# A hybrid encoder layer on one core: the order of the first gated units, the tiles for copies of x, and the queues of the far stretch

## The chip, the cores and the metric

The kernel runs on one core of a Trainium2 chip. The metric is the time of one execution on the device, in microseconds (us). The core has a matrix engine (TensorE, PE in the profile), three engines for the rest (VectorE or DVE, ScalarE or ACT, GpSimd or POOL) and SyncE (SP), which here only issues transfers. A transfer (DMA) is issued by the queue of one engine, in that queue's order, and moved by 16 DMA engines that all queues share.

## The reference

One layer over 2048 tokens of width 1024, all in float32:

```python
y = rmsnorm(x, norm_mix_g) @ w_in            # 512 q, 512 k, 512 v, 512 a, 512 g
att  = dilated_sliding_attention(rotary(q), rotary(k), v)   # 8 heads of 64; dilations 1, 4, 16
conv = silu(layernorm(conv31(a * sigmoid(g))))              # depthwise, 31 taps
h = x + concat(att, conv) @ w_out
xq, xk, xv = rmsnorm(h) @ w_xq, rmsnorm(mem) @ w_xk, rmsnorm(mem) @ w_xv   # 256 memory rows
h = h + cross_attention(xq, xk, xv) @ w_xo                  # 4 heads of 256
h = h + square(relu(rmsnorm(h) @ w_up)) @ w_down            # 4096 wide
out = rmsnorm(h, norm_final_g)
```

The attention takes three patterns (windows of 128, 512 and 2048 tokens at dilations 1, 4 and 16), each a softmax over a band, and joins them by their log-denominators.

## The kernel before, in words

Tokens are taken in four blocks of 512 (`n` or `p` = 0 to 3), channels in tiles of 128. Products are made exact enough by splitting each operand into a high and a low part: three matmuls (lines 263 to 265, `mm3`) for each product, into one PSUM bank of 128 x 512.

The order in which each engine takes its instructions is made by a planner: it takes the program's order as priority and issues what its own timing says is ready, so work may come earlier than it is written. Python generators interleave the stages (`weave(main, (side, rate))` takes `rate` steps of a side for each step of the main one; `pipeline` runs weight loads and splits of later units ahead). `after(stack, name)`, and `behind` and `pinned` that use it, put what is traced inside behind the last instruction kept under that name: "pe" is the last matmul, "dve" a VectorE instruction, "sumsq" ScalarE's sum of squares, "x0_7" the ScalarE cast (line 406) of tile 7 of block 0. The edge is made by `tc.issue_after` and orders instructions within a queue; it waits for no result.

**The first stage.** `xprep(sp, n)` (line 386) loads a block of x in its natural layout, sums squares on ScalarE (line 375), makes the factor of the norm, and then, for each of eight channel tiles, transposes it on TensorE (line 400), copies it out (VectorE, line 402, into a tile `xts` with three buffers), writes the copy to DRAM (`xscr`, on SyncE's queue; it is wanted far later), scales it (`xv`, VectorE, line 405), casts it to f16 (`xh`, ScalarE, line 406) and subtracts (`xl`, GpSimd, line 407). `glu_first` (line 631) runs the first gated pair, channel tile 0 of g and a, over blocks 0 and 1. Per unit it loads 128 columns of `w_in`, squares them, scales, casts, subtracts (`wscale` and `scaled_split`: lines 202, 219, 220, 221), and runs 24 matmuls per block (8 channel tiles by 3). The other pairs for blocks 0 and 1 come from `glu`, then the q and k units (`lin_qk`, which need the scales made in `qkscale` from all of w_in's q and k columns) and the v unit (`lin_v`). `edges` writes zeros to the ends of two arrays in DRAM, `memory` prepares the 256 memory rows.

**The far stretch** (about 450 to 770 us) runs attention for block 0, all three patterns, of which the one with dilation 16 (`att_far`, line 1000 on) covers all tokens. Beside it `filler` runs the gated pairs for blocks 2 and 3 and `Matrices`, which makes the cross-attention's k and v projections (`proj`), the scores' matrices (`turn`, `score`) and the back projections (`back`), each from weights loaded in order into two buffers (`raw_m`, line 461). Attention parks its parts in DRAM (`oscr`) and reads them again in `combine`. Weights and attention's keys, queries and values are loaded on SyncE's queue; results (`kscr`/`vscr` of the projections, `ascr`, `bscr`, `oscr`) are written on GpSimd's. After 124 steps of attention (50 and 74) the rest of the filler is drained, then `backs`, the back projections and the first two w_out tiles, run alone; then `post(0)` starts, with attention's last steps woven in.

Of the kernel before, what the change touches and what calls it, by code (L numbers as in the profile page):

```python
# [21 lines left out]
P = 128  # L22
# [25 lines left out]
def hybrid_layer(ctx, tc, A, out):  # L48
# [338 lines left out]
    def xprep(sp, n):  # L387
        xtiles(n)
        nat = [load_nat(sp, A["x"][0, 512 * n + P * j:512 * n + P * (j + 1), :], f"xn{n}_{j}", q=nc.gpsimd if n > 1 else None) for j in range(4)]
        yield  # L390
        r = rstd_nat(sp, nat, f"x{n}")
        rb = ps("c", f"rb{n}")
        bcast_rows(rb, r, 4)
        rbs = sp.tile([P, 512], F32, tag="rbs", name=f"rbs{n}", bufs=1)
        ACT.copy(rbs, rb)
        yield
        for k in range(KC):
            pt = ps("a", f"xt{n}_{k}")
            for j in range(4):
                PE.transpose(pt[:, j * P:(j + 1) * P], nat_cols(nat[j], k), ident)  # L400
            xt = sp.tile([P, 512], F32, tag="xt", name=f"xts{n}_{k}", bufs=3)
            DVE.tensor_copy(xt, pt)
            dma(xscr[k][:, 512 * n:512 * (n + 1)], xt)
            xv = sp.tile([P, 512], F32, tag="xv", name=f"xv{n}_{k}", bufs=2)
            DVE.scalar_tensor_tensor(xv, pt, gmix[:, k:k + 1], rbs, op0=ALU.mult, op1=ALU.mult)
            last[f"x{n}_{k}"] = ACT.copy(XH_[k, n], xv)
            POOL.tensor_tensor(XL_[k, n], xv, XH_[k, n], op=ALU.subtract)
            yield
# [5 lines left out]
    def memory(sp):  # L414
# [7 lines left out]
        ACT.copy(gm, pm[:, 0:8])  # L422
        mh, ml = ([sp.tile([P, 4, NMEM], F32R, tag=f"m{q}{i}", name=f"m{q}{i}") for i in range(2)] for q in "hl")
        for k2 in range(KC // 2):
# [18 lines left out]
    class Matrices:  # L443
# [8 lines left out]
        def load(self, i):  # L452
            if i >= 32:
                return
            raw = wp.tile([P, 8, P] if i < 24 else [P, 2, 512], F32, tag="raw", name=f"raw_m{i}", bufs=2)
            if i < 24:
                src = wcols((w_xk, w_xv, w_xq)[i // KC], i % KC * P)
            else:
                h, nh = divmod(i - 24, 2)
                src = w_xo[256 * h:256 * h + 256, 512 * nh:512 * nh + 512].rearrange("(e p) m -> p e m", p=P)  # L460
            dma(raw, src)
            self.ring[i] = raw
# [20 lines left out]
        def gather(self, x, h):  # L483
            t = self.part(f"mvm{h}", f"{x}t{h}", (P, 2, 2, NMEM))
            for q in range(2):
                dma(f(t[:, q]), f(pscr[x][q, 2 * h:2 * h + 2].rearrange("e p m -> p e m")))
            return t

        def proj(self, i):
# [16 lines left out]
            for q in range(2):  # L506
                dma(f(pscr[x][q, j]), f(t[q]), nc.gpsimd)
            if i == 15:
# [22 lines left out]
        def score(self, h):  # L531
            kt, wt = self.kt, self.wt
            for k2 in range(4):
                pt = ps("mm", f"pa{h}{k2}")
                for q in range(2):
                    k = 2 * k2 + q
                    for e in range(2):
# [5 lines left out]
                                  self.rbm.unsqueeze(1).to_broadcast([P, 2, NMEM]), op=ALU.mult)  # L543
                dma(ascr[h // 2, :, 2 * k2:2 * k2 + 2, h % 2, :], e3, nc.gpsimd)
                if k2 == 3:
# [3 lines left out]
        def back(self, i):  # L549
# [4 lines left out]
            for mc in range(2):  # L554
# [4 lines left out]
                if mc == 0:  # L559
# [3 lines left out]
                dma(bscr[4 * nh:4 * nh + 4, :, 2 * h + mc, :].rearrange("m p c -> p m c"),  # L563
                    ev.rearrange("p (m c) -> p m c", c=P), nc.gpsimd)
                yield
# [33 lines left out]
    def glu(c, ns, fine=False):  # L599
# [4 lines left out]
        def unit(x, c0):  # L604
            raw = wlin("raw", f"{x}{c}{ns[0]}")
            dma(raw, wcols(w_in, c0))
            yield
# [22 lines left out]

    def glu_first(c, ns):

        raw, w, sig = {}, {}, {}
        c0 = {"g": 3 * DATT + DCONV + c * P, "a": 3 * DATT + c * P}
        for x in "ga":
            raw[x] = wlin("raw", f"{x}{c}{ns[0]}")
            dma(raw[x], wcols(w_in, c0[x]))
            yield
        for x in "ga":
            yield from wscale(raw[x], f"{x}{c}", 1 if x == "g" else 0)  # L640
            w[x] = wlin("whi", f"{x}{c}{ns[0]}"), wlin("wlo", f"{x}{c}{ns[0]}")
            scaled_split(raw[x], kept_scale[f"{x}{c}"][0], *w[x], POOL)
            yield
        DVE.tensor_scalar(cwu[:, c], cw[:, c], kept_scale[f"a{c}"][1], None, op0=ALU.mult)
        for n in ns:
            for x in "ga":
                pt = ps("mm", "lin")
                for _ in linear_steps(pt, *w[x], n):
                    yield
                if x == "g":  # L650
                    sig = t2(f"sig{c}_{n}")
                    ACT.activation(sig, pt, AF.Tanh, scale=kept_scale[f"g{c}"][1])
                else:
                    u = t2(f"u{c}_{n}")
                    last["dve"] = DVE.scalar_tensor_tensor(u, sig, 1.0, pt, op0=ALU.add, op1=ALU.mult)
                    dma(uscr[c][:, 15 + 512 * n:15 + 512 * (n + 1)], u)
                yield
# [24 lines left out]
    def lin_v(hook):  # L682
# [4 lines left out]
        def load(e):  # L687
            raws[e] = wp.tile([P, 8, P], F32, tag="raw", name=f"raw_v{e}", bufs=2)
            dma(raws[e], wcols(w_in, 2 * DATT + P * e))

# [203 lines left out]
    with ExitStack() as st:  # L894
        sp = pool("stage", stack=st)
        setup()
        pair = glu_first(0, (0, 1))
        x0, x1 = xprep(sp, 0), xprep(sp, 1)
        next(x0)
        next(pair)  # L900
        next(x1)
        next(pair)
        next(x0)
        for _ in range(3):
            behind("sumsq", pair)
        drain(x0)
        for _ in range(3):
            behind("x0_7", pair)
        early01 = (0, 1)
        units = [pair] + [u for c in range(1, 4) for u in glu(c, early01)]  # L910
        units += [lin_qk(isq, c) for c in ("r", 0, 1, 2) for isq in (False, True)]
# [93 lines left out]
    def att_far(p2_, h, k, vt, q, start=0):  # L1005
# [7 lines left out]
        def unit(rq):  # L1013
# [96 lines left out]
    def att_units(p, far, then):  # L1110
# [25 lines left out]
        def unit(pr, hh, pat, g, k, q_, opt, o0):  # L1136
# [139 lines left out]
    with ExitStack() as st:  # L1276
# [55 lines left out]

        drain(pinned(backs(), "pe"))

# [637 lines left out]
```

## Time and profile before

| | us |
|---|---|
| median of 3 runs | 2873.29 |
| fastest and slowest of these | 2869.66 and 2874.86 |
| the profiled execution | 2869.13 |
| its span in the trace | 2867.3 |
| TensorE busy in the span | 2709.2 |
| VectorE, ScalarE, GpSimd busy | 1902.0, 1274.5, 538.1 |

A group of the profile reads: line, engine, operation, the tile written and the tiles read, shapes, count, then busy time and mean nanoseconds of one, then the engine's idle time just before them and what ended it. A row of the timeline is start, duration, engine, line, operation, and in brackets the idle time before it with its cause. A row of the waits is who waited for whom: us in total, times, longest. SPq and POOLq are the issues of DMAs on SyncE's and GpSimd's queues. Rows by stages give, for each stretch, busy time and count of each engine, the granted TensorE clock, the share of the DMA engines and GB/s.

### The profile page before, as it was taken

How to read it: one execution, taken by the hardware profiler on the slowest of the kernel's cores; microseconds unless marked ns; L12 is line 12 of the kernel's file. 1: busy time of each engine (PE TensorE's matmuls, PEld its weight loads, DVE VectorE, ACT ScalarE, POOL GpSimd, SP SyncE). 2: the span in 40 equal slices, each digit the busy share in tenths (PEclk: the TensorE clock that was granted, in tenths of full speed). 3: DMA queues.
4: the chain of work that ended last, by engine and by line, in shares of the span. 5: the costliest groups of instructions: out<-in, count | busy, mean ns of one | idle time of the engine just before them, and what ended most of it. 6: DMA issues, size and time to landing. Idle time of an engine off the chain costs nothing.

```text
span 2867.3 us, 40621 instructions
## 1 busy us (share of the span) xinstructions
PE 2709.2 (94%) x14783; PEld 2082.4 (73%) x14783; DVE 1902.0 (66%) x3475; ACT 1274.5 (44%) x2171; POOL 538.1 (19%) x744
## 2 busy tenths in 40 slices
PE   4999999879789999999999999999999999999998
PEld 2544447666577787878888888888888788878877
DVE  3548835555379876568897478866474776666665
ACT  4753215645435433433554534454343544444335
POOL 3545302332200221220210201111020122200000
PEclk8999999999899999999999999999999999999999
DMA  8665537776643666676547766775533554485553
GB/s 239 196 171 113 141 103 216 209 220 181 218 144 118 211 224 204 220 230 213 184 144 239 238 216 219 223 231 176 182 120 121 169 202 164 151 306 162 173 180 103
DMA packets 488096, 535.68 MB, mean 187 GB/s; under 512 B 81637, under 2 KB 361817, under 8 KB 487896
## 3 DMA queue, kind: packets, MB, share of 16 engines
q1 hardware_dynamic: 457360, 434.94, 50.5%
q0 software_dynamic: 28688, 94.82, 9.2%
q10 hardware_dynamic: 1848, 3.33, 0.3%
q8 instruction: 116, 1.90, 0.3%
q14 instruction: 84, 0.69, 0.1%
HBM read 384.46 MB, written 148.52 MB: 186 GB/s over the span
## 4 chain that ended last, share of the span: by engine, by line
PE 65%; issue 10%; DVE 8%; DMA 8%; ACT 3%; POOL 3%; SPq 2%; POOLq 0%; ACTq 0%; DVEq 0%
PE b L1670 7%; PE dn L263 4%; PE dn L264 4%; PE dn L265 4%; PE up L263 3%; PE up L265 3%; PE up L264 3%; PE pt L962 2%; SPq L57 2%; DVE cacc L280 2%; PE s L1155 2%; PE x L264 1%; PE x L263 1%; PE x L265 1%; PE lin L263 1%
## 5 line engine op out<-in xcount | busy, mean ns | idle before, releaser
L280 DVE SCALAR_TENSOR_TENSOR cacc<-cu,cwu,cacc 128x512 f32<-128x512 f32 x480 | 396.8, 828 | 6.4
L956 ACT ACTIVATE sm<-sm,o 128x256 f32<-128x256 f32 (+1 forms) x384 | 160.4, 467 | 125.2 <-DVE o L955 124.9
L263 PE MATMUL dn<-hhh,whi_d 128*128 128x512 f32 x512 | 201.6, 404 | 3.6 <-ACT hhh L1507 2.6
L263 PE MATMUL up<-mh,whi_u 128*128 128x512 f32 x512 | 203.9, 398 | 0.0
L264 PE MATMUL dn<-hhl,whi_d 128*128 128x512 f32 x512 | 199.7, 393 | 0.8 <-DVE hhl L1508 0.8
L265 PE MATMUL up<-mh,wlo_u 128*128 128x512 f32 x512 | 200.0, 391 | 0.0
L264 PE MATMUL up<-ml,whi_u 128*128 128x512 f32 x512 | 199.7, 390 | 0.0
L265 PE MATMUL dn<-hhh,wlo_d 128*128 128x512 f32 x512 | 198.9, 391 | 0.0
L955 DVE CUSTOM_DVE_ANT_0 sm<-s,mask 128x256 f32<-128x256 f32 (+1 forms) x384 | 127.2, 375 | 35.2 <-PE s L1155 13.7
L966 DVE TENSOR_TENSOR pl<-pt,ph 128x512 f16<-128x512 f32 x160 | 109.8, 686 | 58.2 <-ACT ph L965 57.6
L1522 DVE TENSOR_TENSOR h<-h,dn 128x512 f32<-128x512 f32 x128 | 86.4, 684 | 70.8 <-PE dn L265 70.3
L241 POOL TENSOR_TENSOR nr<-st_v,mhalf 128x4 f32<-128x4 f32 x12 | 13.5, 1127 | 629.1 <-DVE st_v L237 629.0
L965 ACT CAST ph<-pt 128x512 f16<-128x512 f32 x160 | 92.6, 579 | 79.8 <-PE pt L962 79.0
L263 PEld LDWEIGHTS dn<-hhh,whi_d 128*128 128x128 f32 x512 | 95.4, 188 | 22.6 <-ACT hhh L1507 3.6
L265 PEld LDWEIGHTS up<-mh,wlo_u 128*128 128x128 f32 x512 | 96.1, 188 | 20.5
L265 PEld LDWEIGHTS dn<-hhh,wlo_d 128*128 128x128 f32 x512 | 96.2, 188 | 20.1
L264 PEld LDWEIGHTS dn<-hhl,whi_d 128*128 128x128 f32 x512 | 96.4, 188 | 19.3 <-DVE hhl L1508 1.6
L264 PEld LDWEIGHTS up<-ml,whi_u 128*128 128x128 f32 x512 | 96.3, 188 | 18.6
L263 PEld LDWEIGHTS up<-mh,whi_u 128*128 128x128 f32 x512 | 96.2, 188 | 18.5
L263 PE MATMUL o<-cath,whi_o 128*128 128x512 f32 x256 | 102.9, 403 | 1.5 <-ACT cath L1104 0.8
L263 PE MATMUL x<-pth,whi_b 128*128 128x512 f32 x256 | 101.1, 401 | 2.4 <-ACT xp L1431 1.5
L263 PE MATMUL xs<-whi_a,yh 128*128 128x512 f32 x256 | 102.3, 401 | 0.0
(586 smaller groups left out, 7965.6 us busy)
## 6 DMA issues: line engine op xcount, KB each, us to landing
raw_u<-in_w_up_dram SPq DMA_DIRECT2D x64, 512.0 KB
raw_d<-in_w_down_dram SPq DMA_DIRECT2D x64, 512.0 KB
k<-kscr SPq DMA_DIRECT2D x32, 640.0 KB
raw_o<-in_w_out_dram SPq DMA_DIRECT2D x32, 512.0 KB
raw_a<-ascr SPq DMA_DIRECT2D x32, 512.0 KB
raw_b<-bscr SPq DMA_DIRECT2D x32, 512.0 KB
lou<-wlo_u POOLq DMA_DIRECT2D x32, 512.0 KB, 5.6
lod<-wlo_d POOLq DMA_DIRECT2D x32, 512.0 KB, 5.6
```

The lines of the kernel that those rows point to most:

```text
L57: (q or nc.sync).dma_start(o, i)
L263: PE.matmul(o, lh, rh, start=first, stop=False)
L264: PE.matmul(o, lh, rl, start=False, stop=False)
L265: last["pe"] = PE.matmul(o, ll, rh, start=False, stop=end)
L280: DVE.scalar_tensor_tensor(acc, u[:, t:t + 512], cwu[:, c, t:t + 1], acc, op0=ALU.mult, op1=ALU.add)
L955: last["dve"] = DVE.tensor_tensor_reduce(dst, so, mask[:, 256 * m:256 * m + nk], 1.0, 3e38, ALU.add, ALU.min, mn)
L956: last["act"] = ACT.activation(dst, dst, AF.Exp, bias=mn, scale=-1.0)
L962: last["pe"] = PE.transpose(pt[:, j, :], sm[:, j, :], ident)
L965: ACT.copy(ph, pt)
L966: DVE.tensor_tensor(pl, pt, ph, op=ALU.subtract)
L1522: last["dve"] = DVE.tensor_tensor(hs[m], hs[m], pt, op=ALU.add)
L1670: PE.matmul(o, w[i][:, k, :], Y[b][q][k], start=first and k + x == 0, stop=k == 3 and x == 2, skip_group_check=not first)
```

## The change

In the first stage, `glu_first` takes both of the first two pairs (g0, a0, g1, a1): it asks for the four weight tiles, the first of them ahead of the first block of x, and runs all four units over block 0 before any runs over block 1. The fourth weight tile lies in a buffer of the `weights` pool, the second pair's split parts in tiles of the stage's own pool, and the memory rows' parts move from that pool to the `weights` pool's split buffers to make room. `xts` has eight buffers instead of three. The steps and rates of the interleaving are set anew; `qkscale` is pinned behind "x1_7"; `edges` is put behind "x3_7", the v weights' and the mask's loads behind "pe".

In the far stretch, the loads of `raw_m`, of the gated pairs for blocks 2 and 3, and of the projections' gathered parts go to GpSimd's queue, and the writes of the projections, scores, back projections and attention's parts to SyncE's. `backs` is woven with attention at 0.55 steps for each of its own instead of running alone.

```diff
-            xt = sp.tile([P, 512], F32, tag="xt", name=f"xts{n}_{k}", bufs=3)
+            xt = sp.tile([P, 512], F32, tag="xt", name=f"xts{n}_{k}", bufs=8)
...
-        mh, ml = ([sp.tile([P, 4, NMEM], F32R, tag=f"m{q}{i}", name=f"m{q}{i}") for i in range(2)] for q in "hl")
+        mh, ml = ([wp.tile([P, 4, NMEM], F32R, tag=f"w{q}", name=f"m{q}{i}", bufs=2) for i in range(2)]
+                  for q in ("hi", "lo"))
...
-            dma(raw, src)
+            dma(raw, src, nc.gpsimd)
...
-                dma(f(t[:, q]), f(pscr[x][q, 2 * h:2 * h + 2].rearrange("e p m -> p e m")))
+                dma(f(t[:, q]), f(pscr[x][q, 2 * h:2 * h + 2].rearrange("e p m -> p e m")), nc.gpsimd)
...
-                dma(f(pscr[x][q, j]), f(t[q]), nc.gpsimd)
+                dma(f(pscr[x][q, j]), f(t[q]))
...
-                dma(ascr[h // 2, :, 2 * k2:2 * k2 + 2, h % 2, :], e3, nc.gpsimd)
+                dma(ascr[h // 2, :, 2 * k2:2 * k2 + 2, h % 2, :], e3)
...
-                    ev.rearrange("p (m c) -> p m c", c=P), nc.gpsimd)
+                    ev.rearrange("p (m c) -> p m c", c=P))
...
-            dma(raw, wcols(w_in, c0))
+            dma(raw, wcols(w_in, c0), nc.gpsimd if fine else None)
...
+    def glu_first(sp, ns):
+
+        units = [(x, c) for c in range(2) for x in "ga"]
+        raw, w, sig = {}, {}, {}
+        for x, c in units:
+            nm = f"{x}{c}"
+            raw[nm] = (wp.tile([P, 8, P], F32, tag="raw", name=f"fraw_{nm}", bufs=2) if nm == "a1" else
+                       wlin("raw", f"{nm}0"))
+            dma(raw[nm], wcols(w_in, 3 * DATT + c * P + (DCONV if x == "g" else 0)))
+            yield
+        for x, c in units:
+            nm = f"{x}{c}"
+            yield from wscale(raw[nm], nm, 1 if x == "g" else 0)
+            w[nm] = [sp.tile([P, 8, P], F16, tag=f"f{q}{nm}", name=f"f{q}_{nm}") if c else wlin(f"w{q}", f"{nm}0")
+                     for q in ("hi", "lo")]
+            scaled_split(raw[nm], kept_scale[nm][0], *w[nm], POOL)
+            if x == "a":
+                DVE.tensor_scalar(cwu[:, c], cw[:, c], kept_scale[nm][1], None, op0=ALU.mult)
+            yield
         for n in ns:
-            for x in "ga":
+            for x, c in units:
                 pt = ps("mm", "lin")
-                for _ in linear_steps(pt, *w[x], n):
+                for _ in linear_steps(pt, *w[f"{x}{c}"], n):
                     yield
...
-            dma(raws[e], wcols(w_in, 2 * DATT + P * e))
+            with ExitStack() as st:
+                after(st, "pe")
+                dma(raws[e], wcols(w_in, 2 * DATT + P * e))
...
-        pair = glu_first(0, (0, 1))
+        four = glu_first(sp, (0, 1))
         x0, x1 = xprep(sp, 0), xprep(sp, 1)
+        next(four)
         next(x0)
-        next(pair)
+        next(four)
         next(x1)
-        next(pair)
+        next(four)
+        next(four)
         next(x0)
         for _ in range(3):
-            behind("sumsq", pair)
+            behind("sumsq", four)
         drain(x0)
         for _ in range(3):
-            behind("x0_7", pair)
+            behind("x0_3", four)
+        behind("x0_5", x1)
+        for _ in range(6):
+            behind("sumsq", four)
         early01 = (0, 1)
-        units = [pair] + [u for c in range(1, 4) for u in glu(c, early01)]
+        units = [four] + [u for c in range(2, 4) for u in glu(c, early01)]
...
-        drain(islice(steps, 10))
-        behind("x0_3", x1)
-        weave(islice(steps, 6), (x1, 1.4))
+        drain(islice(steps, 6))
+        weave(islice(steps, 24), (x1, 0.5))
         drain(x1)
         later = pinned(chain(xprep(sp, 2), xprep(sp, 3), memory(sp)), "x1_7")
-        qks = qkscale()
-        weave(islice(steps, 16), (later, 0.25), (qks, 0.25))
-        weave(islice(steps, 11), (later, 2.4), (qks, 0.7))
+        qks = pinned(qkscale(), "x1_7")
+        weave(islice(steps, 34), (later, 0.4), (qks, 0.2))
+        weave(islice(steps, 7), (later, 2.4), (qks, 0.7))
         drain(later, qks)
-    edges()
+    with ExitStack() as st0:
+        after(st0, "x3_7")
+        edges()
...
-    dma(mask, A["masks"])
+    with ExitStack() as st0:
+        after(st0, "pe")
+        dma(mask, A["masks"])
...
-                dma(oscr[pr][1].rearrange("(p r) (h e) -> p r h e", r=16, h=2)[:, 4 * rq - 4:4 * rq + 4, hh], o2,
-                    nc.gpsimd)
+                dma(oscr[pr][1].rearrange("(p r) (h e) -> p r h e", r=16, h=2)[:, 4 * rq - 4:4 * rq + 4, hh], o2)
...
-                    os_.rearrange("p b h e -> p b (h e)"), nc.gpsimd if far else nc.scalar)
+                    os_.rearrange("p b h e -> p b (h e)"), None if far else nc.scalar)
...
-        drain(pinned(backs(), "pe"))
+        weave(pinned(backs(), "pe"), (first, 0.55))
```

More of the change, by code (lines that the diff above doesn't have):

```diff
@@ L629, in glu @@
         return unit("g", 3 * DATT + DCONV + c * P), unit("a", 3 * DATT + c * P)
-    def glu_first(c, ns):
+    def glu_first(sp, ns):
+        units = [(x, c) for c in range(2) for x in "ga"]
         raw, w, sig = {}, {}, {}
-        c0 = {"g": 3 * DATT + DCONV + c * P, "a": 3 * DATT + c * P}
-        for x in "ga":
-            raw[x] = wlin("raw", f"{x}{c}{ns[0]}")
-            dma(raw[x], wcols(w_in, c0[x]))
-            yield
[L639 to L642, printed above, removed]
+        for x, c in units:
[3 more added lines that the diff above has]
+            dma(raw[nm], wcols(w_in, 3 * DATT + c * P + (DCONV if x == "g" else 0)))
+            yield
+        for x, c in units:
[6 more added lines that the diff above has]
+                DVE.tensor_scalar(cwu[:, c], cw[:, c], kept_scale[nm][1], None, op0=ALU.mult)
             yield
-        DVE.tensor_scalar(cwu[:, c], cw[:, c], kept_scale[f"a{c}"][1], None, op0=ALU.mult)
         for n in ns:
-            for x in "ga":
+            for x, c in units:
                 pt = ps("mm", "lin")
-                for _ in linear_steps(pt, *w[x], n):
+                for _ in linear_steps(pt, *w[f"{x}{c}"], n):
                     yield
```

## The prediction

> **What bounds the kernel now.** I read the page first, then the busy time by stages, then the waits of the engine that is busiest, and then the order of time where that engine stood still. Busy columns are TensorE, its weight loads, VectorE, ScalarE, GpSimd; after them the granted clock, the DMA share and GB/s.
>
> ```profile
> span 2867.3 us, 40621 instructions
> ```
>
> ```profile
> 24.00:84.00 60.00, 36.97 (x168) 20.07 (x166) 26.29 (x55) 30.73 (x66) 31.86 (x36) 0.83 0.79 221
> 84.00:100.00 16.00, 13.47 (x62) 6.61 (x61) 5.97 (x10) 13.87 (x36) 6.75 (x6) 0.89 0.57 170
> 100.00:165.00 65.00, 60.54 (x312) 31.85 (x311) 35.80 (x81) 41.08 (x72) 30.34 (x28) 0.97 0.68 181
> 165.00:450.00 285.00, 274.90 (x1294) 129.89 (x1293) 177.83 (x217) 81.00 (x106) 100.08 (x122) 0.99 0.54 144
> 450.00:720.00 270.00, 236.05 (x2269) 189.19 (x2268) 154.72 (x549) 153.03 (x345) 82.60 (x121) 0.96 0.71 197
> 720.00:800.00 80.00, 54.36 (x287) 41.05 (x284) 29.71 (x70) 30.81 (x51) 13.48 (x18) 0.86 0.73 226
> ```
>
> TensorE bounds it nearly everywhere. The holes are in the two stages that the change edits: 23.0 us from 24 to 84 us, and 34.0 plus 25.6 us in the far stretch (450 to 800). Between 100 and 450 us only 14.6 of 350 us are idle: whatever is won ahead of that can be kept there, since TensorE only has to start its queue sooner. Time is won by filling holes, not by removing arithmetic: the change removes no matmul.
>
> The early hole, in order of time on VectorE, TensorE and SyncE's queue:
>
> ```profile
> 44.86 0.69 DVE L402 COPY xts<-xt 128x512 f32<-128x512 f32 x1 [15.41 <-DMA xscr<-xts]
> ...
> 46.35 1.94 PE L400 MATMUL xt<-ident,xn 128*128 128x128 f32 x8 [13.80 <-DVE xv L405]
> ...
> 21.42 13.20 SPq L57 DMA_DIRECT2D uscr<-zero  x8
> 34.66 0.43 SPq L57 DMA_DIRECT2D raw_v<-in_w_in_dram  x1
> 37.31 0.33 SPq L57 DMA_DIRECT2D mask<-in_masks_dram  x1
> 37.74 0.38 SPq L57 DMA_DIRECT2D xscr<-xts  x1
> ```
>
> VectorE's sixth copy of x needs the tile of the third, there being three. That tile's write to DRAM stands on SyncE's queue behind eight writes of zeros, a v weight and the mask, is issued at 37.74 and lands shortly before 44.86. VectorE waits 15.41 us, and TensorE, behind VectorE, 13.80.
>
> **The change part by part.** *Eight tiles for the copies.* All eight copies of x's first 512 tokens then have a tile of their own, so the 13.80 us go, whatever SyncE's queue does. What is late next: the second 512 tokens reuse the tiles, and their third copy needs the write of 37.74; it comes no sooner than about 44, so little is left of that wait. Term: -13.8.
>
> *Two gated pairs over tokens 0 to 511 first, then over 512 to 1023.* What TensorE does per matmul at full clock, and what the other engines need per tile and per unit of weights:
>
> ```profile
> 78.61 0.38 PE L265 MATMUL lin<-xh,lwlo_a 128*128 128x512 f16 x1
> 78.82 0.60 PE L400 MATMUL xt<-ident,xn 128*128 128x128 f32 x4
> 79.26 0.38 PE L263 MATMUL lin<-xh,lwhi_g 128*128 128x512 f16 x1
> ```
>
> ```profile
> 24.00:84.00 60.00, 28.20 (x98) 0.69 (x1) 1.06 (x2) 0.83 0.79 221
> ```
>
> ```profile
> L407 POOL TENSOR_TENSOR xl<-xv,xh 128x512 f16<-128x512 f32 x16 | 18.4, 1163 | 17.4 <-ACT xh L406 17.2
> L400 PE MATMUL xt<-ident,xn 128*128 128x128 f32 x64 | 12.5, 337 | 15.8 <-DVE xv L405 15.7
> L405 DVE SCALAR_TENSOR_TENSOR xv<-xt,gmix,rbs 128x512 f32<-128x512 f32 x16 | 11.6, 744 | 4.3 <-ACT rbs L395 2.3 <-POOL xl L407 1.9
> L402 DVE COPY xts<-xt 128x512 f32<-128x512 f32 x16 | 11.0, 688 | 25.8 <-DMA xscr<-xts 15.4 <-PE xt L400 10.3
> ...
> L219 ACT ACTIVATE lraw_g<-lraw_g,wscl 128x1024 f32<-128x1024 f32 x2 | 2.3, 1141 | 1.3 <-DVE sqv_g L189 1.3
> ...
> L221 POOL TENSOR_TENSOR lwlo_a<-lraw_a,lwhi_a 128x1024 f16<-128x1024 f32 x1 | 2.1, 2128 | 0.6 <-ACT lwhi_a L220 0.6
> ```
>
> From 78.61 to 78.82 a matmul takes 0.21 us, and four transposes 0.44. The second of these fences counts the gated matmuls alone: 98 by 84 us, beside 64 transposes. After the change 96 gated matmuls (four units of 24) need only the first 512 tokens: 96 x 0.21 + 16 x 0.44 = 27.2 us. The first gated matmul came at 24.54; one of the x loads will be later for the weight ahead of it, so I start at 25.5 and reach 52.7. Holes that stay: the second unit's weights are squared, scaled, cast and subtracted (some 1.1 us each on ScalarE, 2.1 on GpSimd, about 5.5 in all) behind x's fourth tile, and the third and fourth units' behind the sums of the next tokens; I put 7 us on them. VectorE's own 16 tiles at 0.74 + 0.69 are 22.9 us from about 22, which ends at 45 and is no bound; GpSimd's 16 x 1.16 + 4 x 2.13 = 27.1 us ends near 52 and is close to one. So the state of 84 us is reached near 60: 24 us sooner, of which 13.8 are counted, 10 more at best and none at worst. I take -7, since every engine is then near its sum. *Weights ahead of x*: half a megabyte at the 221 GB/s of that stage is 2.4 us for the first x load (bounds 0 and +2.4, the sums of squares having slack elsewhere): +1.
>
> *The q and k scales' sums, held on ScalarE behind the second 512 tokens' last tile.* They are also asked for later in the order of the work.
>
> ```profile
> L740 ACT ACTIVATE qks<-qks x16: 616/628/632, 72.2 to 133.8; 128x512 f32<-128x512 f32 x16
> ```
>
> They spread over 62 us now. Begun at 60 and spread alike they end at 122; the q and k units that need them would like to start 20 us sooner than now. Nothing at best, +8 if they slip by an eighth of their spread: +2.
>
> *Three edits that I cost at nothing: edge zeros behind "x3_7", mask and v weights behind "pe".* Such a name holds a ScalarE or TensorE instruction, while these blocks issue on SyncE and VectorE. The profile shows what such a hold does, since the preparation of x's third 512 tokens is held behind "x1_7" already:
>
> ```profile
> 26.14 0.72 POOL L57 DMA_DIRECT2D xn<-in_x_dram  x1
> ...
> 76.26 0.62 ACT L406 CAST xh<-xv 128x512 f16<-128x512 f32 x1 [0.64 <-DVE xv L405]
> 76.78 0.62 ACT L375 ACTIVATE junk<-xn 128x512 bf16<-128x512 f32 x1
> ```
>
> The cast at 76.26 is x1_7. ScalarE's sums follow it at once, but the loads were issued on GpSimd's queue 50 us ahead of it: a hold binds only its own engine. The zeros, mask and v weights go on filling SyncE's early gaps. If the holds did bind, 13.2 us of SyncE's queue would move from 21 us to near 130: -3 to +5.
>
> *The far stretch's queues.* 40 weight loads (32 of cross-attention, 8 gated) and 16 gathers go to GpSimd's queue; 32 projections, 16 score, 16 back and 20 attention writes go to SyncE's. The two longest waits of GpSimd's queue there, two of the stretches in which TensorE idles (columns as above), and TensorE's own waits from 720 on:
>
> ```profile
> POOL oscr L57 <- ACT o L1034: 50.5, 9, 13.1
> POOL bscr L57 <- ACT eb L562: 34.3, 13, 8.9
> ```
>
> ```profile
> 610.00:620.00 10.00, 2.73 (x10) 1.86 (x11) 3.81 (x11) 2.14 (x5) 1.43 (x8) 0.50 0.69 178
> ...
> 790.00:800.00 10.00, 1.83 (x16) 1.15 (x16) 8.93 (x29) 1.60 (x4) 0.00 (x0) 0.71 0.76 216
> ```
>
> ```profile
> PE pb L263 <- ACT eb L562: 17.0, 6, 6.6
> PE opt L970 <- DMA v<-vtok: 6.2, 1, 6.2
> ```
>
> ```profile
> DMA to landing us min/median/max: 2.7/4.6/8.1
> ```
>
> The last row is the time from issue to landing of the back projections' writes. For it: a weight no longer queues on SyncE behind the loads of the concatenation. Against it: 84.8 us of waiting for results (and more for the scores) move in front of attention's key, query and value loads. GpSimd waited in the same order and with the same slack, and loses as many issues as it gains, so its combines (which run in order behind its DMAs) see one kind of wait for another. Bounds: -13 (the ten microseconds at 610 and one value wait, less than whole) to +50.5; nearest row is TensorE's single value wait of 6.2 us, small and already there, so 0.
>
> The trace gives the DMA share as 0.71 in this stretch and 0.73 in the next. The Trainium skill, DMA: Bandwidth & Descriptors, section Rules for kernel authors, says that spreading transfers over issuing engines brings no bandwidth and saves only issue time; by that rule this term is 0 as well, and the head-of-queue waits are what can make it differ.
>
> *Attention's last steps woven into the back projections at 0.55 per step.* About 25 steps take some 13 of attention, which is nearly all that is left. TensorE idles 17.0 us in the back projections, waiting for ScalarE, which waits for the write of two tiles before (landing 4.6 us); attention fills part of it, and the 8.2 us hole at 790, where the last combine and a value load are awaited, loses the combine. Bounds 0 and -25; half of the hole and a third of the waits is -10.
>
> Sum: -13.8 - 7 + 1 + 2 + 0 - 10 = -27.8. The profiled execution took 2869.13 (its span and 1.83 around it), so 2841.3; the median of the runs is 4.2 above that execution, so 2845.
>
> **The rivals.** *A, slower: SyncE holds attention's loads behind its new writes.* Place: 450 to 720. The waits for the far output (50.5) stand at the head of SyncE's queue, and each delays the next head's keys and the single-buffered values. If all of it reached TensorE: 2845 + 50.5 = 2895. It decides from 28 us, 55% of that row. For it: the queue is served in order. Against: TensorE is busy for 236 of 270 us there, which leaves slack, and these writes are ready before the next head starts.
>
> *B: the early gain is lost again.* If q and k start no sooner, because the scale sums, ScalarE (13.87 busy of 16 us at 84) or GpSimd set the pace, about 6 of the 18 stay, and with 0 to -10 from the back projections: 2857 to 2867.
>
> *C, about even or slower: weights on GpSimd land late.* A transfer from there lands between 2.7 and 8.1 us after issue; 3.5 above the median on each of 24 later matrices is 84, of which two buffers hide at least half: 2845 + 42 = 2887.
>
> The Trainium skill, SBUF — State Buffer, section SBUF: two separate sides, names a cause for C: some VectorE copies lock GpSimd out while it writes descriptors. No run here shows it yet.
>
> *D, faster: the swap also fills the idle stretches of the far stage:* 2845 - 13 - 5 = 2827.
>
> **How the numbers follow.** The forecast 2845 (2834 to 2857) has 0.42, D 0.15, B 0.20 (a third of it within 0.2%, 5.7 us, about what a measurement can tell from no change), A 0.13, C 0.07, smaller mixtures 0.03, of which 0.01 is within 0.2%. Faster: 0.42 + 0.15 + 0.13 + 0.02 = 0.72; same 0.08; slower 0.20. The range from 2822 to 2884 leaves out A, half of C and the end of D, about 0.2.
>
> **What would show it.** Right: no wait of VectorE for xscr before 60 us; x1_7 cast near 60 instead of 76.26; 98 gated matmuls by 60; zeros still on SyncE ahead of 60; TensorE idle under 12 us in the back projections. Wrong: value or key waits of TensorE of tens of microseconds from 450 to 720 (A), ScalarE waiting for raw_m (C), or idle TensorE between 100 and 200 (B).

## The result, and the profile after

The changed kernel takes 2827.32 us (median of 4 runs, 2822.73 to 2827.61), against 2871.47 for the kernel before beside it (4 runs, 2868.08 to 2874.86): a ratio of 0.9842, 95% interval 0.9825 to 0.986. That is some 45 us less, where 28 were forecast: near the fast end of the range from 2822 to 2884, and faster than the 2834 to 2857 around the forecast.

The span and the busy time by stages, in the same six stages as in the prediction:

```profile
span 2825.5 us, 40587 instructions
...
24.00:84.00 60.00, 50.35 (x247) 26.12 (x248) 28.69 (x66) 39.60 (x82) 37.35 (x38) 0.97 0.87 246
84.00:100.00 16.00, 16.00 (x85) 8.43 (x84) 7.20 (x19) 15.97 (x42) 6.70 (x7) 1.00 0.63 210
100.00:165.00 65.00, 56.43 (x273) 29.71 (x271) 35.80 (x61) 36.53 (x57) 30.09 (x32) 0.92 0.77 190
165.00:450.00 285.00, 278.17 (x1392) 137.28 (x1391) 183.68 (x261) 87.46 (x133) 108.04 (x123) 0.99 0.53 145
450.00:720.00 270.00, 233.01 (x2207) 186.42 (x2206) 152.55 (x528) 151.79 (x335) 70.71 (x98) 0.94 0.76 211
720.00:800.00 80.00, 73.31 (x379) 59.36 (x378) 54.84 (x95) 40.73 (x63) 1.44 (x2) 0.96 0.73 214
```

TensorE is busy for 50.35 of the first 60 us instead of 36.97, with 247 matmuls instead of 168; part of it is lost again between 100 and 165 (8.6 us idle instead of 4.5). The last row compares different work, since all of it begins earlier. For the far stretch it is better to compare landmarks: the first start of attention's transposes, of the back projections, of the output projection, and of the score products behind it. They are read from rows like these two, of before and of after (count, shortest, median and longest ns, first and last start):

```profile
L962 PE MATMUL pt<-ident,sm x640: 269/272/477, 456.8 to 1947.8; 128*128 128x128 f32 x160
```

```profile
L978 PE MATMUL pt<-ident,sm x640: 269/273/422, 438.5 to 1901.7; 128*128 128x128 f32 x160
```

| kernel (label) | first `pt` | first `pb` | first `o` | first `xs` | span | `pt` to `pb` | `pb` to `xs` |
|---|---|---|---|---|---|---|---|
| before | 456.8 | 721.7 | 768.2 | 834.6 | 2867.3 | 264.9 | 112.9 |
| after | 438.5 | 690.5 | 746.6 | 791.8 | 2825.5 | 252.0 | 101.3 |
| e1_early | 440.3 | 702.7 | 751.6 | 816.1 | 2845.1 | 262.4 | 113.4 |
| e2_tiles8 | 448.5 | 712.7 | 760.0 | 825.1 | 2859.9 | 264.2 | 112.4 |
| e3_queues | 453.6 | 707.0 | 752.5 | 817.4 | 2853.9 | 253.4 | 110.4 |
| e4_weave | 461.4 | 726.3 | 787.2 | 832.3 | 2867.4 | 264.9 | 106.0 |
| e5_loads | 457.0 | 721.8 | 766.2 | 831.6 | 2862.9 | 264.8 | 109.8 |
| e6_writes | 452.1 | 698.7 | 741.0 | 806.1 | 2843.1 | 246.6 | 107.4 |
| e7_after_tiles3 | 442.2 | 691.8 | 748.1 | 793.3 | 2827.7 | 249.6 | 101.5 |
| e8_after_bscr_act | 435.1 | 689.7 | 746.3 | 795.5 | 2834.2 | 254.6 | 105.8 |
| e9_writes_only | 439.3 | 685.8 | 742.6 | 790.4 | 2824.6 | 246.5 | 104.6 |
| e10_writes_bind | 445.8 | 689.9 | 744.8 | 789.8 | 2827.6 | 244.1 | 99.9 |
| e11_oscr | 458.2 | 720.4 | 764.8 | 830.2 | 2867.0 | 262.2 | 109.8 |
| e12_xwrites | 458.0 | 714.2 | 758.7 | 823.5 | 2855.6 | 256.2 | 109.3 |

So of the change's 42.8 us by the score products, 18.3 are there when attention starts, 12.9 are won up to the back projections, and 11.6 from there on. After that nothing more is won: the span is 41.8 us shorter. Each row is one profiled execution. Single landmarks of kernels that share their first stage differ by up to 9 us (452.1 to 461.4 where that stage was not edited), and the stretch behind the score products, where no edit lies, takes 2029.0 to 2038.7 us; so a few microseconds are decided by the ratios.

### The profile page after: what moved, and what is told of

It is laid out like the page before. It is cut to its first block, busy times and chain, and to the rows that moved or that the text cites. A ratio compares the mean times of both kernels' runs of the same rounds, so it can differ in the third digit from the quotient of the medians.

```text
span 2825.5 us, 40587 instructions
## 1 busy us (share of the span) xinstructions
PE 2697.4 (95%) x14783; PEld 2075.6 (73%) x14783; DVE 1898.2 (67%) x3475; ACT 1272.6 (45%) x2171; POOL 525.7 (19%) x716
## 4 chain that ended last, share of the span: by engine, by line
PE 69%; DMA 9%; issue 8%; DVE 6%; ACT 4%; POOL 2%; SPq 1%; ACTq 0%; POOLq 0%; DVEq 0%
PE b L1685 7%; PE dn L263 4%; PE dn L264 4%; PE dn L265 4%; PE up L263 3%; PE up L265 3%; PE up L264 3%; PE lin L263 2%; PE lin L265 2%; PE lin L264 2%; PE pt L978 2%; PE s L1170 2%; SPq L57 1%; PE x L264 1%; PE x L263 1%
## 5 line engine op out<-in xcount | busy, mean ns | idle before, releaser
L265 PEld LDWEIGHTS up<-mh,wlo_u 128*128 128x128 f32 x512 | 96.2, 188 | 20.4
```

The lines of the kernel that those rows point to most:

```text
L265: last["pe"] = PE.matmul(o, ll, rh, start=False, stop=end)
```

## The experiments

**The first stage alone.** First all of the first stage's edits on the kernel before, then only the tiles of the copies.

```diff
+            xt = sp.tile([P, 512], F32, tag="xt", name=f"xts{n}_{k}", bufs=8)
+        four = glu_first(sp, (0, 1))
...
```

> The first stage of the change alone (two pairs, weights ahead of x, eight copy tiles, the new interleaving), with the far stretch's queues and the back projections as before. My theory: attention's first transpose comes about 18 us sooner (456.8 before, 438.5 in the changed kernel) and all of it reaches the end: 2871 - 18 = 2853. Rival (the far stretch takes it back, since its DMA waits set its pace): 2862 or more.

```diff
-            xt = sp.tile([P, 512], F32, tag="xt", name=f"xts{n}_{k}", bufs=3)
+            xt = sp.tile([P, 512], F32, tag="xt", name=f"xts{n}_{k}", bufs=8)
```

> Only the eight tiles for the copies of x, on the kernel before. My theory by the prediction's term: 13.8 us less, 2857, since TensorE's 13.80 us wait goes and the work that follows is bound by TensorE. Rival: the wait is replaced by others (one pair has only 48 matmuls per block to fill with), 5 us or less, 2866 to 2871.

Measured: the whole first stage 0.9932 (0.9914 to 0.995), about -19.5 us; the eight tiles alone 0.9958 (0.9942 to 0.9974), about -12. VectorE's longest wait up to 100 us and the busy time of the early stretch of e2_tiles8, then the busy time of e1_early, whose first row is TensorE alone up to 69 us:

```profile
DVE xts L402 <- PE xt L400: 22.7, 14, 7.4
```

```profile
24.00:84.00 60.00, 44.81 (x193) 23.23 (x192) 29.56 (x61) 40.27 (x89) 36.09 (x38) 0.83 0.84 246
```

```profile
24.00:69.00 45.00, 35.43 (x167) 0.96 0.86 230
...
24.00:84.00 60.00, 50.43 (x244) 26.25 (x245) 28.29 (x64) 39.09 (x81) 37.35 (x38) 0.97 0.86 243
```

The tiles remove the wait for DRAM (VectorE now waits for TensorE's transposes), and bring TensorE from 36.97 to 44.81 us busy; the other edits of the first stage (the two pairs, the weights ahead of x, the held scales, the new interleaving) bring the rest, to 50.43. No run separates these from each other, and by the ratios their gain beside the tiles, some 7.5 us, is not clear of the noise (the two intervals overlap). The 168 matmuls that the kernel before had done by 84 us are done near 69. The same edit taken out of the changed kernel:

```diff
-            xt = sp.tile([P, 512], F32, tag="xt", name=f"xts{n}_{k}", bufs=8)
+            xt = sp.tile([P, 512], F32, tag="xt", name=f"xts{n}_{k}", bufs=3)
```

> The changed kernel with three tiles for the copies of x instead of eight. If the copies' wait is as bad as before, 12 to 14 us more: 2840. Rival (the second pair's weights give TensorE enough to do meanwhile, or the order of the first stage hides it): within 4 us of 2827.

Measured: 0.9881 (0.9866 to 0.9895), so about 11 us of the change's gain go by the ratios, 6.5 by the medians (2833.83 against 2827.32). Of e7_after_tiles3, VectorE's waits up to 100 us, and the early stretch:

```profile
DVE xts L402 <- DMA xscr<-xts: 11.6, 2, 11.2
```

```profile
24.00:84.00 60.00, 42.96 (x208) 23.12 (x209) 25.20 (x59) 31.85 (x60) 35.16 (x37) 0.91 0.76 212
```

The wait for the copy's write is back, 11.2 of the former 15.41 us, and with it 7.4 us of TensorE. By the landmarks of this one profiled execution, the fastest of its four, attention starts at 442.2, only 3.7 us later than in the changed kernel; the ratios say more, with intervals whose ends allow 2 to 20. Both ratios put the tiles near 12 us, with the second pair beside them or without.

**The weave alone.**

```diff
-        drain(pinned(backs(), "pe"))
+        weave(pinned(backs(), "pe"), (first, 0.55))
```

> Only the weaving of the back projections with attention at 0.55, on the kernel before. By the prediction's term 10 us less, 2861; in the changed kernel the stretch from the first back projection to the first score product took 11.6 us less. Rival: it only moves the idle time (the back projections take 55.8 instead of 46.3 us), 2869 to 2873.

Measured: 0.9965 (0.9947 to 0.9983), about -10 us. The two parts of the back projections' stretch, split at the first output projection, of before and of e4_weave:

```profile
722.00:768.00 46.00, 28.98 (x96) 21.07 (x95) 9.69 (x12) 18.39 (x26) 11.42 (x15) 0.81 0.76 241
768.00:835.00 67.00, 57.39 (x308) 46.05 (x307) 43.72 (x92) 29.27 (x49) 2.06 (x3) 0.90 0.62 185
```

```profile
726.00:787.00 61.00, 40.03 (x205) 29.80 (x202) 21.03 (x59) 27.04 (x46) 11.97 (x16) 0.80 0.76 241
787.00:832.00 45.00, 44.75 (x208) 36.86 (x209) 32.85 (x46) 20.21 (x29) 1.50 (x2) 1.00 0.64 191
```

```profile
PE pb L263 <- ACT eb L562: 17.4, 6, 5.2
```

The 96 matmuls that filled the first part have become 205, but the idle time in it has not shrunk (17.0 before, 21.0 now), and the wait of the back projections for ScalarE is 17.4 us as it was 17.0. What is gone are the 9.6 idle us of the second part. So in this trace the weave pays behind the back projections, not in the waits beside which it was put. The trace shows a part of the 10 us only: this execution is the slowest of its ten (2869.21 against a median of 2856.92) and no faster than the kernel before. Its stretch from attention's first transpose to the score products is 6.9 us shorter (370.9 instead of 377.8), but it starts 4.6 us later.

**The queues.** The whole exchange on the kernel before, then its two halves:

```diff
+            dma(raw, src, nc.gpsimd)
+                dma(f(t[:, q]), f(pscr[x][q, 2 * h:2 * h + 2].rearrange("e p m -> p e m")), nc.gpsimd)
+            dma(raw, wcols(w_in, c0), nc.gpsimd if fine else None)
...
+                dma(f(pscr[x][q, j]), f(t[q]))
+                dma(ascr[h // 2, :, 2 * k2:2 * k2 + 2, h % 2, :], e3)
+                    ev.rearrange("p (m c) -> p m c", c=P))
+                dma(oscr[pr][1].rearrange("(p r) (h e) -> p r h e", r=16, h=2)[:, 4 * rq - 4:4 * rq + 4, hh], o2)
+                    os_.rearrange("p b h e -> p b (h e)"), None if far else nc.scalar)
```

> Only the exchange of queues in the far stretch (weights and gathers to GpSimd, results' writes to SyncE), on the kernel before. The landmarks of the changed kernel say 13 us from attention's first transpose to the first back projection, so 2858; the prediction's term was 0, 2871; rival A of the prediction would make it slower than 2877.

The first three lines alone:

> On the kernel before, only half of the exchange: weights and gathers of the far stretch to GpSimd's queue, the results' writes stay there too. My theory (the gain of 15 us comes from taking weights out of SyncE's queue, where they stand behind value loads): most of it, 2856 to 2860. Rival (the gain comes from the writes leaving GpSimd's queue, whose waits held the combines): 2866 to 2871, or slower, since GpSimd's queue then carries both.

The last five alone:

> On the kernel before, the other half: only the results' writes to SyncE's queue, weights stay there too. My theory: no gain, or a loss of up to 10 us, 2868 to 2880, since SyncE then carries everything and its head waits for results. Rival (writes leaving GpSimd make the gain): 2854 to 2860.

Measured: the exchange 0.9948 (0.9931 to 0.9965), about -15 us; the loads alone 0.9997 (0.9984 to 1.0011), nothing; the writes alone 0.9921 (0.9901 to 0.9942), about -23. My theory, that the loads carry the gain, fell. Of the 18.3 us that e6_writes gains from the first `pt` to the first `pb`, 16.4 come after the first `xqt`, the first transpose of the scores' weights (140.9 us before, 124.5 now). Most of them lie at one wait. Of before, the busy time between the first score and the first back projection and all that TensorE waits for there, then VectorE and TensorE in order of time:

```profile
595.00:722.00 127.00, 106.53 (x1007) 83.15 (x1007) 69.34 (x238) 59.30 (x138) 37.24 (x58) 0.93 0.67 188
```

```profile
PE xqt L522 <- issue: 11.9, 1, 11.9
PE opt L972 <- DVE pl L966: 4.3, 1, 4.3
PE xqt L522 <- DVE wlo_m L525: 4.3, 4, 1.8
```

```profile
615.00 0.17 DVE L1066 TENSOR_TENSOR csm<-ld 128x8 f32<-128x8 f32 x1 [11.61 <-DMA ld<-oscr]
...
615.64 0.68 DVE L525 TENSOR_TENSOR wlo_m<-xqt,whi_m 128x512 fp32r<-128x512 f32 x1
```

```profile
603.86 0.60 PE L522 MATMUL xqt<-ident,raw_m 128*128 128x128 f32 x4
...
616.42 1.08 PE L522 MATMUL xqt<-ident,raw_m 128*128 128x128 f32 x4 [11.86 <-issue]
```

The combine of attention's parts (`csm`) reads them back from DRAM. VectorE reaches it 22.6 us after the first `xqt`, stands 11.61 us, and behind it in the same order stands the low half of a transposed weight (`wlo_m`, L525), without which TensorE goes no further: a hole of 11.86 us. The profile names no releaser for that hole (it says issue); that it is `wlo_m` is read from the order of time, the next `xqt` starting 0.10 us after `wlo_m` ends. Of e6_writes, the same stretch, its combine, and all that TensorE waits for there:

```profile
588.00:699.00 111.00, 104.10 (x1013) 82.09 (x1010) 69.06 (x238) 58.94 (x139) 18.83 (x34) 0.98 0.81 214
```

```profile
597.60 0.17 DVE L1065 TENSOR_TENSOR csm<-ld 128x8 f32<-128x8 f32 x1 [0.76 <-DMA ld<-oscr]
```

```profile
PE xqt L522 <- DVE wlo_m L525: 4.7, 4, 1.8
PE opt L972 <- DVE pl L966: 1.1, 1, 1.1
PE xqt L522 <- PE s L1154: 1.0, 1, 1.0
```

VectorE reaches the combine at the same distance (596.8, 22.6 after `xqt` at 574.2) and finds the data 0.76 us later; the hole is gone, TensorE's wait for VectorE's `pl` falls from 4.3 to 1.1, and idle time falls from 20.5 of 127 us to 6.9 of 111. With the loads moved alone, GpSimd's queue still stands before the writes of the parts, and the combine waits longer (e5_loads):

```profile
POOL oscr L57 <- ACT o L1034: 38.8, 8, 13.6
```

```profile
DVE csm L1066 <- DMA ld<-oscr: 14.9, 2, 13.8
```

And in the whole exchange the loads put a new head of queue on GpSimd, each waiting for the buffer that VectorE's split frees (e3_queues):

```profile
POOL raw_m L57 <- DVE wlo_m L255: 89.7, 13, 27.6
```

The Trainium skill, DMA: Bandwidth & Descriptors, section Rules for kernel authors, has spreading over issuing engines save issue time alone. For the loads the runs agree (0.9997). The gain of the writes is of another kind: the trace has it in waits, above all for the parts read back, and of such waits that rule says nothing.

**Which of the writes.** The parts of attention alone, and all others alone, on the kernel before:

```diff
+                dma(oscr[pr][1].rearrange("(p r) (h e) -> p r h e", r=16, h=2)[:, 4 * rq - 4:4 * rq + 4, hh], o2)
+                    os_.rearrange("p b h e -> p b (h e)"), None if far else nc.scalar)
```

> The kernel before with one kind of write moved to SyncE's queue: attention's partial results, which VectorE's combine reads back. Theory (the gain of the moved writes is that these partial results stand no longer behind waiting work on GpSimd, and the combine's wait of 11.6 us goes): the larger part of the gain of all the writes, ratio 0.993 to 0.995, first transpose to first back projection near 250 us instead of 264.9. Rival (the gain is from the far stretch's results leaving GpSimd): ratio 0.999 to 1.000 and that stretch still near 264.

```diff
+                dma(f(pscr[x][q, j]), f(t[q]))
+                dma(ascr[h // 2, :, 2 * k2:2 * k2 + 2, h % 2, :], e3)
+                    ev.rearrange("p (m c) -> p m c", c=P))
```

> The kernel before with the complement: the far stretch's results (keys, values and the scales' factors that are written to be gathered again) are written on SyncE's queue, attention's partial results stay on GpSimd's. Theory (the partial results carry the gain): ratio 0.998 to 1.000, at most 5 us, the combine's wait for its partial results still over 10 us. Rival (the far stretch's results carry it): ratio 0.992 to 0.994, some 20 us, and first transpose to first back projection near 247 us.

Measured: the parts alone 1.0001 (0.9992 to 1.0011), nothing; the others alone 0.9966 (0.9955 to 0.9978), about -10 us. Neither makes the 23 us, and my theory fell with its rival. VectorE's wait at the combine, first of e11_oscr, then of e12_xwrites (the profile names no releaser for these, which it calls issue):

```profile
612.44 0.17 DVE L1065 TENSOR_TENSOR csm<-ld 128x8 f32<-128x8 f32 x1 [9.74 <-issue]
```

```profile
611.26 0.17 DVE L1066 TENSOR_TENSOR csm<-ld 128x8 f32<-128x8 f32 x1 [8.31 <-issue]
```

In these kernels VectorE reaches the combine 22.6 us after the first `xqt` (23.4 in e5_loads). Whether it has to wait there is decided by two times: when the second read of the parts is issued on SyncE's queue, and how long it then takes until the combine starts. All times in us; DMA share is that between the read's issue and the combine's start (it can read over 1), and e9_writes_only is the changed kernel with its loads back on SyncE's queue, of which more below:

| kernel (label) | read issued after first `xqt` | issue to combine | DMA share | VectorE waits | TensorE's hole | first `xqt` to first `pb` |
|---|---|---|---|---|---|---|
| e5_loads | 33.9 | 3.3 | 0.51 | 13.8 | 14.3 | 147.5 |
| before | 24.4 | 9.8 | 0.95 | 11.6 | 11.9 | 140.9 |
| e11_oscr | 21.4 | 11.0 | 0.95 | 9.7 | 10.0 | 140.3 |
| e12_xwrites | 22.2 | 8.8 | 0.95 | 8.3 | 8.6 | 133.9 |
| e3_queues | 20.4 | 8.6 | 1.10 | 6.4 | 6.6 | 137.8 |
| after | 20.3 | 8.3 | 1.10 | 6.0 | 6.2 | 136.0 |
| e9_writes_only | 18.4 | 5.4 | 0.83 | 1.2 | 1.4 | 124.4 |
| e6_writes | 18.2 | 5.2 | 0.82 | 0.8 | none | 124.5 |

The wait of VectorE and the hole of TensorE go together in all eight, and the stretch is shortest where both are gone; it is not the hole alone that shortens it (e12_xwrites against e11_oscr). Moving both kinds of writes brings the read forward and lets it land sooner than either alone. It lands in 3.3 to 5.4 us where the DMA engines are at 0.51 to 0.83, and in 8.3 to 11.0 where they are at 0.95 or more. That points to the load on the DMA engines; no run here changes that load alone, so the cause of the slow landing stays open.

**The back projections' hole in the changed kernel.** Of after, TensorE's waits from 690 to 835 us, ScalarE and SyncE's queue in order of time:

```profile
PE pb L263 <- ACT eb L563: 21.2, 3, 14.5
```

```profile
700.00:710.00 10.00, 0.00 (x0) 0.00 (x0) 0.00 (x0) 0.00 (x0) 0.18 (x1) 0.54 1.05 401
```

```profile
711.81 1.45 ACT L563 ACTIVATE eb<-pb,rmem 128x512 f32<-128x512 f32 x2 [13.42 <-DMA bscr<-eb]
```

```profile
692.44 1.10 SPq L57 DMA_DIRECT2D cath<-cath  x2
...
703.93 0.32 SPq L57 DMA_DIRECT2D catl<-catl  x1
705.86 1.85 SPq L57 DMA_DIRECT2D bscr<-eb  x2
```

For ten microseconds nearly nothing runs while the DMA engines are full; the writes of the back projections come on SyncE's queue behind 14 transfers of the concatenation. I put these writes on ScalarE's queue:

```diff
-                    ev.rearrange("p (m c) -> p m c", c=P))
+                    ev.rearrange("p (m c) -> p m c", c=P), nc.scalar)
```

> The changed kernel with the back projections' results (bscr) written on ScalarE's queue, so that they don't stand behind the sixteen loads of the concatenation on SyncE's queue. In the changed kernel ScalarE waits 13.4 us there for the first write, and TensorE 14.5 us. My theory: that wait goes, 8 to 14 us less, 2813 to 2819. Rival (attention's woven steps fill the time anyway, or the loads of the concatenation keep the DMA engines busy, whatever the queue): within 4 us of 2827.

Measured: 0.9874 (0.9851 to 0.9897), no gain over the change's 0.9842. The wait is spread and 6.3 us less, not gone (e8_after_bscr_act, the same view):

```profile
PE pb L263 <- ACT eb L563: 14.9, 7, 4.5
```

And the stretch from the first back projection to the score products takes 105.8 us instead of 101.3. So my theory fell: the place in the queue wasn't the whole cause. That the full DMA engines are the rest was only argued.

**The writes without the loads, and holds that bind.** In the changed kernel the three holds of the first stage (zeros, mask, v weights) hold nothing back: the zeros are issued at 23.69 us, the mask at 36.78 and the v weights at 40.92 and 60.55, though the cast that "x3_7" names comes at 146.7. Without the three holds, every engine and queue has the same instructions in the same order. On the changed kernel, first the loads back on SyncE's queue, then the holds made to bind as well, on SyncE's own writes of the copies:

```diff
-            dma(raw, src, nc.gpsimd)
+            dma(raw, src)
...
```

> The changed kernel with one thing undone: the far stretch's weights and gathered halves are loaded on SyncE's queue again, only the result writes stay on SyncE's queue as in the change. Theory (the moved writes bring the gain and the moved loads cost some of it: on the kernel before, the writes alone gave a ratio of 0.9921 and the whole exchange 0.9948): about 7 us below the changed kernel, 2817 to 2822, ratio 0.981 to 0.983, and the stretch from attention's first transpose to its first back projection near 246 us instead of 252. Rival (beside the early start and the woven back projections SyncE's queue carries too much, and its writes stand behind loads that wait): 2827 or more, ratio 0.984 or above, with the normalizer's write of a back projection still more than 5 us behind its issue order.

```diff
+            last[f"w{n}_{k}"] = nc.sync.dma_start(xscr[k][:, 512 * n:512 * (n + 1)], xt)
...
-        after(st0, "x3_7")
+        after(st0, "w1_7")
...
-        after(st0, "pe")
+        after(st0, "w3_7")
```

> As the kernel of the run before, and the three holds of the first stage made to bind: the zeros and attention's first weights of v are issued on SyncE's queue behind the write of the second block's copy, the mask behind the write of the fourth. Theory (what the holds put off is wanted by nobody before 100 us, and the freed share of the queue is under 13 us of transfers): the same as the run before within 5 us, the second block's cast perhaps 3 us earlier than 74. Rival (the early stretch waits on DMA, which the 9.0 us of waits for x's loads would say): attention's first transpose 5 to 9 us earlier, ratio lower by 0.002 to 0.003.

Measured: the loads back, 2820.3 us, 0.983 (0.9813 to 0.9846); with binding holds, 2828.4, 0.9863 (0.9848 to 0.9878). The first has the stretch up to the back projections at 246.5 us, as forecast from e6_writes, but gives 3.3 us back behind them (104.6 instead of 101.3) and starts attention 0.8 later; its interval overlaps that of the change, so it is the lowest median here and not shown to be faster. What the loads take is seen at the same hole, first of after, then of e9_writes_only: the change has closed only half of it.

```profile
PE xqt L523 <- issue: 6.2, 1, 6.2
```

```profile
PE xqt L523 <- issue: 1.4, 1, 1.4
```

The second is slower than the first by 8.1 us by the medians and 9.5 by the ratios, which neither theory nor rival had. Of e10_writes_bind, the early stages, SyncE's zeros, and the waits of ScalarE and TensorE from 84 to 105 us:

```profile
24.00:84.00 60.00, 52.35 (x250) 27.26 (x251) 28.64 (x66) 39.54 (x81) 36.95 (x38) 0.94 0.66 190
84.00:100.00 16.00, 10.86 (x54) 5.17 (x52) 1.15 (x4) 5.94 (x17) 2.13 (x1) 0.93 0.78 218
```

```profile
74.79 13.64 SPq L57 DMA_DIRECT2D uscr<-zero  x8
```

```profile
ACT qks L748 <- DMA qks<-in_w_in_dram: 10.0, 1, 10.0
```

```profile
PE xt L400 <- DVE xv L405: 6.9, 1, 6.9
```

Up to 84 us the freed queue gives TensorE 2 us (52.35, and 50.16 in e9_writes_only). Then the zeros stand at 74.79 for 13.64 us in front of the loads for the q and k scales; ScalarE waits 10.0 us for these, VectorE for ScalarE, and TensorE 6.9 for VectorE (10.86 us busy from 84 to 100, and 16.00 in e9_writes_only). Attention starts 6.5 us later. But these two executions are level again at the score products (789.8 and 790.4), and their spans differ by 3.0 us only, which come later still. So the early loss is shown, and that it makes the 8 to 9.5 us is not. No reason is left to make the holds bind.

## Why the prediction was right or wrong

The parts measured alone add up: e1_early, e3_queues and e4_weave multiply to 0.9846, the change is 0.9842. They come to -19.5, -15 and -10, where the prediction had -17.8, 0 and -10. So nearly all that the sum was off by is one term.

- **Eight tiles, -13.8:** right, in size and in place. Alone -12; taken out of the change, +7 to +11; VectorE's wait for the write goes and comes back with it.
- **Two pairs, weights ahead of x, scales, -7 + 1 + 2 = -4:** not contradicted; e1_early less e2_tiles8 is some -7.5, not clear of the noise. But the working was too hopeful inside: of the 96 gated matmuls that it had done by 60, 74 are, and 96 by 66; the state of 84 us comes near 69, not near 60, and is 15 us sooner rather than 24. With the tiles counted the term gave -17.8 by attention's start, and 18.3 were measured. So the -7 did better than the chain that led to "near 60"; it was a guess, and that it fitted is partly luck.
- **x1_7's cast near 60 instead of 76.26:** wrong, with no harm. The second 512 tokens are now prepared at a lower rate beside the units of the first, and that cast comes at 74.28, while TensorE has work all the same. No wait of VectorE for `xscr` is left, as forecast.

Of after, VectorE's longest wait up to 100 us, that cast, and the zeros and the mask on SyncE's queue:

```profile
DVE xts L402 <- PE xt L400: 23.3, 13, 9.8
```

```profile
74.28 0.62 ACT L406 CAST xh<-xv 128x512 f16<-128x512 f32 x1 [0.69 <-DVE xv L405]
```

```profile
23.69 13.05 SPq L57 DMA_DIRECT2D uscr<-zero  x8
36.78 0.43 SPq L57 DMA_DIRECT2D mask<-in_masks_dram  x1
```

- **Three holds, 0:** right. They bind nothing. Binding ones, measured beside e9_writes_only, cost 8 to 9.5 us, beyond the end of +5 that I gave them; I had looked at what the zeros free and not at what they would stand in front of later.
- **Queue exchange, 0 (bounds -13 and +50.5):** this is the step that failed; it measured about -15 alone (-10 to -20 by its interval), with -13 as its best case in the prediction. I took the ten microseconds at 610 as an upper bound of a gain and then chose 0 by the row of a value wait of 6.2 us. The row to choose by was in the trace: VectorE's 11.61 us for the parts read back, in the same ten microseconds, with TensorE's 11.86 behind it. I also took it that GpSimd's combines "see one kind of wait for another"; the combine that mattered was VectorE's, which waits for a read on SyncE's queue, and the order and landing of that read changed with the writes.
- **Weave, -10:** right in size (-10 alone), wrong in place, and so in part by luck. I gave it half of the hole at 790 and a third of the waits in the back projections. By its trace it took the whole of the first and nothing of the second: TensorE's wait for ScalarE there is 21.2 us in the changed kernel, where I had put under 12.
- **Rivals.** A (SyncE's queue holds attention's loads) did not happen: with all the writes on SyncE TensorE waits less than before. B did not happen: 18.3 us were there at 438.5, and none was lost up to 791.8. C (weights late) did not cost time by itself (e5_loads), though beside the moved writes the loads seem to cost some 8 us (e3_queues against e6_writes, intervals that overlap); the place that the traces single out for it is VectorE's combine, not a weight. D is what came nearest, at a chance of 0.15: the swap does gain in the far stretch. That 2827 and 2827.32 agree so closely is luck: D gave the swap -18 where -15 were measured, the first stage made up for part of it (-19.5 where -17.8 were forecast), and of the hole of 11.86 us that D took as filled, 6.2 still stand in the changed kernel.

## What to carry to other kernels

Where an engine runs its work in a written order, look in its waits for a small instruction that waits on data read back from DRAM, and see what stands behind it: 11.6 us of a combine on 128 by 8 numbers cost TensorE 11.9. Which queue the writes stand on mattered here (0.9921), where the queue's head waits for other results; which queue the prefetched loads stand on changed nothing by itself here, and seemed to cost some microseconds beside the moved writes. And before moving an early transfer out of the way, see what it will stand in front of at its new place.

## What the runs showed that was not expected

The two kinds of writes don't add: 0 and -10 us apart, -23 together. The loads of 512 KB cost GpSimd 884 to 927 ns of issue each, against a median of 384 on SyncE's queue. The rows of the same eight loads, in e3_queues and in e6_writes:

```profile
L57 POOL DMA_DIRECT2D raw_m<-in_w_xv_dram x8: 884/897/927, 467.5 to 538.6; - x8
```

```profile
L57 SPq DMA_DIRECT2D raw_m<-in_w_xv_dram x8: 372/384/640, 467.0 to 541.4; - x8
```

The granted clock of TensorE between the first score and the first back projection was 0.93 where 20.5 of 127 us were idle and 0.98 where 6.9 of 111 were; with it, the busy time of about 1010 matmuls fell from 106.53 to 104.10 us. In this stretch a filled hole so came with 2.4 us less busy time as well. The same two go together in e11_oscr (0.93 and 106.41 us) and e12_xwrites (0.96 and 104.26).
